# A hybrid encoder layer in split fp32: the norm moved from x to the columns, on GpSimd

## The chip, the cores and the metric

The kernel runs on one core of a Trainium2 chip. The metric is the device time of one execution in microseconds (us), as the median of several runs. TensorE (PE) multiplies matrices, VectorE (DVE) and ScalarE (ACT) work element by element, GpSimd (POOL) does the same more slowly and issues DMAs of its own, SyncE (SP) issues most of the others. Each engine takes its instructions strictly in the order in which the program lists them.

## What is computed

One layer, 512 tokens, 2048 channels, 12 heads in three branches (A forgetting attention, B chunked attention, C stick-breaking attention), all in float32:

```python
hn = rmsnorm(x, norm_g)                      # x * rsqrt(mean(x*x) + EPS) * norm_g
proj = einsum('bsd,dc->bsc', hn, w_in)       # 12 x (q, k, v, gate), 4 forget logits, 3 x 2048 gate columns
f_logit = proj[..., QKVG_COLS:QKVG_COLS + N_HEADS] + b_f
gates = sigmoid(proj[..., QKVG_COLS + N_HEADS:] + b_gate)
# A: q, k normed per head; logits + c[q] - c[k], c = cumsum(log_sigmoid(f_logit)); causal softmax
# B: q, k normed; learned bias by distance; softmax over a band
# C: causal, weights exp(z + sum of log(1 - beta) over the keys between)
ys = heads * silu(gate path)
up = einsum('bsnw,nwd->bsnd', ys, w_up)
out = x + einsum('bsd,de->bse', sum(gates * up), w_out)
```

The row factor rsqrt(mean(x*x) + EPS) of a token multiplies every column of that token's projection alike, so it can be put on x or on the columns. norm_g belongs to the channel, which is summed over, and has to be on x (or on the weights).

## The kernel before

Tokens lie on the free axis, channels or columns on the 128 partitions. A float32 operand is split in two parts that TensorE takes at full rate: hi is a rounded copy (ScalarE, `split`), lo the rest (VectorE). A product is hi x hi + hi x lo + lo x hi. A column block (128 columns of w_in) has 16 channel tiles (k-tiles), each with three matmuls over 512 tokens: 48 matmuls.

Most column blocks are computed in twos (`PairTask`) by Strassen's scheme with seven products instead of eight. A product is a unit: 8 matmuls of weights hi over 512 columns (hi and lo of half the tokens side by side) and 8 of weights lo over 256. It needs sums of weight quarters (two by VectorE, two by a DMA that GpSimd issues and that adds to the tile it writes, `add_up`, L278) and sums and differences of x quarters (`combos`). A pair's first form of product order is called late: it asks for the combinations of x as late as possible.

The order of the stages is this. x comes in 16 tiles; VectorE or ScalarE multiplies each by norm_g (`prep_x`, L422, L425), then it is split. With these the first head's four blocks, q, k, v and gate of (C, 0), are made plainly (`first_quad`), k-tile by k-tile, with one more matmul per k-tile and part for the forget logits (weights `w2`, 8 columns: hi and lo of four). Meanwhile ScalarE sums the squares of x (read again with tokens on the partitions, `norm_x`, L455), and one fp32 matmul (L470) spreads the row factors over all partitions (`rstd`). VectorE then multiplies x by rstd and splits it once more (`split_n`, L490); the quad's columns are multiplied by rstd as they leave PSUM (L1205). Four gate columns follow plainly (`col_task`), and during them VectorE and ScalarE make the combinations of x. From there on all is pairs: for each of eleven heads a q, k pair and a v, gate pair, between them pairs of gate columns (stored to memory, `spill`, and read back at the end), and the heads' attention in between. In branch A the running sum of the log forget gates is laid in two tiles (`forget_sums`), and a matmul per query block (L980) adds its differences to the logits. At the end come the up projections (units of w_up), the merge with the gates, and eight pairs of w_out.

The order of instructions on PE, ACT and DVE is written out by a planner (`Flow`): tasks are generators that yield an engine, an assumed cost and a due time, and the planner emits whichever can start first, then the one due first. POOL and SP instructions before the change keep an order of their own that a scheduler sets. Weight tiles: six raw ones (`NR`), splits made two units ahead (`LA`).

Of the kernel before, what the change touches and what calls it, by code (L numbers as in the profile page):

```python
# [15 lines left out]
P = 128  # L16
# [13 lines left out]
NEG = -1e30  # L30
SCALE = HD ** -0.5
# [4 lines left out]
PE, ACT, DVE = 0, 1, 2  # L36
# [26 lines left out]
class Flow:  # L63
# [5 lines left out]
    LATE = (0.3, 0.12, 0.12)  # L69

    def __init__(self):
        self.clock = [0.0] * 3
        self.idle = [0.0] * 3
        self.now = self.fin = 0.0
        self.tasks = []
# [84 lines left out]

@with_exitstack
def hybrid_kernel(
# [4 lines left out]
    consts: bass.AP,  # L167
    w_col: bass.AP,
# [152 lines left out]
    ohf = cp.tile([P, NH], F32, name="ohf")  # L321
    nc.gpsimd.memset(ohf, 0.0)
    for r in range(4):
        nc.gpsimd.affine_select(out=ohf[32 * r:32 * r + 32, :], in_=ohf[32 * r:32 * r + 32, :],
                                pattern=[[1, NH]], base=0, channel_multiplier=-1,
                                compare_op=ALU.not_equal, fill=1.0)

    gq = cp.tile([P, 4], F32, name="gq")
    nc.vector.tensor_copy(gq, gqk)
    for c in (0, 2):  # L330
        nc.vector.tensor_scalar_mul(gq[:, c:c + 1], gqk[:, c:c + 1], SCALE)

    w2 = cp.tile([P, KT, 2 * NH], F32R, name="w2")
    nc.vector.tensor_copy(w2[:, :, :NH], wf)
    nc.vector.tensor_sub(w2[:, :, NH:], wf, f(w2[:, :, :NH]))
# [4 lines left out]
                                                  mybir.EngineType.DVE}))  # L340
# [56 lines left out]
    norm_ev = [Event() for _ in range(KT)]  # L397
    used_q = [Event() for _ in range(KT)]
    used_g = [Event() for _ in range(UK)]
    x1 = [Parts("x1", [norm_ev[k], Event()]) for k in range(UK)]  # L400
    x2 = [Parts("x2", [norm_ev[k + UK]] * 2) for k in range(UK)]
# [5 lines left out]
    atts.free.pop()  # L407
    xps.free.clear()


    xnat = [xp.tile([P, 2, S], F32, tag="x", name=nm("xn")) for _ in range(UK)]
# [3 lines left out]
    def prep_x(kt):  # L415

        due = (5.0 + 3.2 * kt,)
        yield x_in[kt]
        x = xraw[kt]
        if kt < 10:  # L420
            yield (DVE, 0.5, *due)
            nc.vector.tensor_scalar_mul(x, x, gn[:, kt:kt + 1])  # L422
        else:
            yield (ACT, 0.65, *due)
            nc.scalar.activation(x, x, AF.Copy, scale=gn[:, kt:kt + 1])  # L425
        yield from split(xs[kt].hi, xs[kt].lo, two(x), S, raw_ev[kt], due, raw_hi[kt])
# [19 lines left out]
    rstd, rstd_ev = [], Event()  # L446
    n_split = [0]

    def norm_x():

        for i in range(NQ * QB):
            yield n_in[i]
            yield ACT, 0.75, 12.0 + 1.5 * i
            x = xnat[i // 2][:, i % 2, :]
            nc.scalar.activation(x, x, AF.Square, accum_out=ssq[:, i // NQ, i % NQ:i % NQ + 1])  # L455
        give(xps, UK)
# [15 lines left out]
        yield t2s, 1  # L472
        yield ACT, act_us(S)
        rstd.append(t2("rstd"))
        nc.scalar.activation(rstd[0], ps, AF.Copy)
# [3 lines left out]
    def rstd_used():  # L479
        n_split[0] += 1  # L480
        if n_split[0] == KT + 5:
            give(t2s)

    def split_n(kt):

        due = (52.0 + 1.0 * kt + (8 if kt >= UK else 0),)
        yield raw_ev[kt]
        yield rstd_ev
        yield (DVE, dve_us(S), *due)
        nc.vector.tensor_mul(xraw[kt], xraw[kt], rstd[0])  # L490
        yield used_q[kt]
        yield from split(xs[kt].hi, xs[kt].lo, two(xraw[kt]), S, norm_ev[kt], due)
        rstd_used()

    def combos(k):

        due = (96.0 + k,)
        late = (106.0 + k,)
        a, b = xraw[k], xraw[k + UK]
        yield norm_ev[k]  # L500
        yield norm_ev[k + UK]
        q = dve_us(HS)
        yield (DVE, q, *due)
        nc.vector.tensor_sub(a[:, LH], a[:, LH], a[:, RH])
        yield (DVE, q, *due)
        nc.vector.tensor_sub(a[:, RH], b[:, RH], a[:, RH])
        yield (DVE, q, *due)
        minus(b[:, RH], b[:, RH], a[:, LH])
        yield (DVE, q, *due)
        minus(b[:, LH], b[:, RH], b[:, LH])  # L510
        yield used_g[k]
        h, lo, ev = x1[k].half(1)
        yield from split(h, lo, a[:, LH], HS, ev, due)
        yield xps, 1
        t23[k] = Parts("t23")
        h, lo, ev = t23[k].half(0)
        yield from split(h, lo, b[:, RH], HS, ev, late)
        h, lo, ev = t23[k].half(1)
        yield from split(h, lo, a[:, RH], HS, ev, late)
        give(t2s)  # L520
# [21 lines left out]

    def col_task(srcs, evac, bank=0, used=None):

        st = {}

        def mms(i):
            def go(u):
                if i == 0:
                    yield accs[bank], 1  # L550
                    st["ps"] = acc(bank)
                ps = two(st["ps"])
                for j in range(UK):
                    kt = i * UK + j
                    yield norm_ev[kt]
                    yield PE, mm_us(S, 2)
                    mm(ps, u.hi[:, j, :], xs[kt].hi, kt == 0)
                    mm(ps, u.hi[:, j, :], xs[kt].lo)
                yield u.ready
                for j in range(UK):  # L560
                    kt = i * UK + j
                    yield PE, mm_us(S)
                    mm(ps, u.lo[:, j, :], xs[kt].hi, stop=kt == KT - 1)
                    if used is not None and i == 0:
                        set_(used[j])
            return go

        def after():
            yield from evac(st["ps"])
            give(accs[bank])  # L570
        return [Unit(mms(i), after if i == 1 else None, srcs=[srcs[i]]) for i in range(2)]
# [20 lines left out]
    class PairTask:  # L592
# [204 lines left out]
    bias, bias_ev, f_ev, f2_ev = {}, Event(), Event(), Event()  # L797
    fd, fd2 = dp.tile([2 * NH, S], F32, name="fd"), dp.tile([NH, S], F32, name="fd2")

    def forget_bias():  # L800
# [5 lines left out]
        nc.sync.dma_start(v, fd[:NH, :].rearrange("h (c t) -> (h c) t", t=T))  # L806
        nc.sync.dma_start(u, fd[NH:, :].rearrange("h (c t) -> (h c) t", t=T))
        yield Event(f_ev.t + 6.0)
        q = 0.15
        yield DVE, q  # L810
        nc.vector.scalar_tensor_tensor(v, v, bfc, u, op0=ALU.add, op1=ALU.add)
        yield DVE, q
# [13 lines left out]
        yield DVE, 3 * q  # L826
        nc.vector.scalar_tensor_tensor(p, p, 1.0, s, op0=ALU.add, op1=ALU.mult)
        nc.vector.tensor_scalar_mul(p, p, 2.0)
        nc.vector.scalar_tensor_tensor(v, v, 0.0, p, op0=ALU.min, op1=ALU.subtract)
        nc.sync.dma_start(fd2.rearrange("h (c t) -> (h c) t", t=T), v)  # L830
        f2_ev.t = flow.fin + 3.0

    def forget_sums():
        yield f2_ev
        yield t2s, 3
        v, s, u = t2("fv"), t2("fs"), t2("fu")
        nc.gpsimd.memset(v, 0.0)
        nc.gpsimd.memset(u, 1.0)
        for r in range(4):
            nc.sync.dma_start(v[32 * r:32 * r + NH, :], fd2)  # L840
        yield Event(flow.now + 6.0)
        yield DVE, 1.2
        nc.vector.tensor_tensor_scan(s, u, v, 0.0, op0=ALU.mult, op1=ALU.add)
        give(t2s)
        yield t2s, 2
        hi, lo = pair_of("c")
        yield from split(hi, lo, s, S)
        give(t2s)
        yield t2s, 2
        crl, crb = t2("crl", F32R), t2("crb")  # L850
        a = ACT, act_us(S)
        yield a
        nc.scalar.activation(crl[0:32, :], f(hi[0:32, :]), AF.Copy)
        yield a
        nc.scalar.activation(crl[32:64, :], f(lo[32:64, :]), AF.Copy)
        yield a
        nc.scalar.activation(crl[64:128, :], u[64:128, :], AF.Copy)
        nc.gpsimd.memset(crb[0:64, :], 1.0)
        yield a
        nc.scalar.activation(crb[64:96, :], f(hi[64:96, :]), AF.Copy, scale=-1.0)  # L860
        yield a
        nc.scalar.activation(crb[96:128, :], f(lo[96:128, :]), AF.Copy, scale=-1.0)
        give(t2s, 3)
        bias["crl"], bias["crb"] = crl, crb
        set_(bias_ev)
# [8 lines left out]
    class Head:  # L874
# [73 lines left out]
        def soft_start(self):  # L948
# [18 lines left out]
        def soft_scores(self, i):  # L967
# [6 lines left out]
            yield PE, mm_us(m, 3) + (mm_us(m) + mm_us(P) if n == A else 0)  # L974
# [4 lines left out]
            if n == A:  # L979
                nc.tensor.matmul(ps, bias["crl"][:, blk(i)], self.bias[:, :m], start=False, stop=False)  # L980
                nc.tensor.matmul(ps[:, blk(i)], identb, mska, start=False, stop=True)
                done = self.nth("s", QB)
                yield DVE, dve_us(m)
# [605 lines left out]
```

## Time and profile before

| | |
|---|---|
| median of 3 runs | 1350.9 us (1350.63 to 1351.42) |
| the profiled execution | 1351.0 us, span from first to last instruction 1349.3 us |
| granted TensorE clock, mean | 0.997 |
| busy: PE, DVE, ACT, POOL | 1326.0, 1108.8, 797.3, 93.5 us |
| first real matmul | 9.96 us |
| quad ends, four plain gate columns end | 64.38, 107.89 us |
| data moved by DMA | 262.00 MB, 194 GB/s on average |

In rows of the profile, L12 is line 12 of the kernel, `out<-in` are the program's tile names, `x16` is a count. In a group's row the busy time and the mean ns of one come first, then the idle time of the engine before them and what ended it. A timeline's row begins with start and length in us. Columns of a windows row: busy time (and instructions) of PE, weight loads, DVE, ACT, POOL, then granted clock, DMA share, GB/s. [...]

### The profile page before, as it was taken

The numbers are of one execution on the slowest core, as the hardware profiler recorded it, in microseconds if no ns is written. First come the engines' busy times: TensorE is split into PE (matmuls) and PEld (weight loads), VectorE is DVE, ScalarE is ACT, GpSimd is POOL, SyncE is SP. The second block draws the span as 40 slices with busy tenths as digits, with TensorE's granted clock in tenths as the row PEclk, the third lists the DMA queues.
The fourth block names the chain that finished last, engine by engine and source line by source line (L and its number), as shares of the span: only waits on it lengthen the run. The fifth ranks groups of instructions, "written<-read, shape, count | busy, mean of one in ns | idle before, by whom it ended". The sixth has DMA issues, their size and how long they took to land.

```text
span 1349.3 us, 19660 instructions
## 1 busy us (share of the span) xinstructions
PE 1326.0 (98%) x7338; PEld 1149.2 (85%) x7338; DVE 1108.8 (82%) x1589; ACT 797.3 (59%) x1224; POOL 93.5 (7%) x123
## 2 busy tenths in 40 slices
PE   7999999999999999999999999999999999989998
PEld 5788888888888888888888888888888788878887
DVE  5998998978878788787888878878787877898786
ACT  6755756656565576655767557665567645454443
POOL 0000000010000000000110000100000000000000
PEclk9999999999999999999999999999999999989999
DMA  9556766667767677777777777777767655758893
GB/s 327 173 143 157 194 171 181 187 195 194 187 196 202 183 212 183 187 204 183 212 174 190 193 194 196 167 193 186 192 184 250 246 192 179 209 134 245 236 250 89
DMA packets 91055, 262.00 MB, mean 194 GB/s; under 512 B 10168, under 2 KB 16440, under 8 KB 90960
## 3 DMA queue, kind: packets, MB, share of 16 engines
q1 hardware_dynamic: 72384, 201.96, 44.6%
q0 software_dynamic: 14976, 54.53, 24.7%
q10 hardware_dynamic: 3600, 4.26, 0.9%
q8 instruction: 57, 0.93, 0.3%
q14 instruction: 38, 0.31, 0.1%
HBM read 241.03 MB, written 19.69 MB: 193 GB/s over the span
## 4 chain that ended last, share of the span: by engine, by line
PE 96%; DVE 3%; DMA 0%; issue 0%; ACT 0%; SPq 0%; DVEq 0%; ACTq 0%
PE acc L262 82%; PE att L262 8%; PE att L1013 1%; DVE wl L247 1%; DVE m L247 1%; PE att L1116 1%; PE att L258 1%; PE att L1117 1%; PE att L259 1%; PE att L257 1%; PE att L1115 1%; DMA x<-in_xT 0%; PE att L1076 0%; PE att L911 0%; PE att L912 0%
## 5 line engine op out<-in xcount | busy, mean ns | idle before, releaser
L247 DVE TENSOR_TENSOR wl<-raw,wh 128x1024 fp32r<-128x1024 f32 (+1 forms) x412 | 494.2, 1200 | 149.7 <-ACT wh L243 148.8
L243 ACT ACTIVATE wh<-raw 128x1024 fp32r<-128x1024 f32 (+1 forms) x412 | 427.1, 1038 | 149.8 <-PE acc L262 69.5
L262 PE MATMUL acc<-x,wh 128*128 128x512 f32 x1600 | 416.1, 396 | 10.0 <-ACT wh L243 10.0
L262 PEld LDWEIGHTS acc<-x,wh 128*128 128x128 f32 x1600 | 287.0, 189 | 62.0 <-ACT wh L243 10.0
L262 PE MATMUL acc<-t,wh 128*128 128x512 f32 x1056 | 272.7, 395 | 0.2 <-ACT wh L243 0.2
L262 PEld LDWEIGHTS acc<-x,wl 128*128 128x128 f32 x1504 | 210.6, 190 | 18.9
L262 PE MATMUL acc<-x,wl 128*128 128x256 f32 (+1 forms) x1504 | 223.7, 289 | 0.0
L262 PEld LDWEIGHTS acc<-t,wh 128*128 128x128 f32 x1056 | 188.0, 189 | 31.9 <-ACT wh L243 0.4
L262 PEld LDWEIGHTS acc<-t,wl 128*128 128x128 f32 x1056 | 145.0, 190 | 11.0
L262 PE MATMUL acc<-t,wl 128*128 128x256 f32 x1056 | 148.6, 282 | 0.0
L278 POOL DMA_DIRECT2D raw<-in_w_col x88 | 76.1, 865 | 934.7 <-DMA raw<-in_w_col 429.1
L262 PE MATMUL acc<-m,wh 128*128 128x512 f32 x448 | 113.8, 396 | 6.4 <-DVE m L247 6.0
L262 PEld LDWEIGHTS acc<-m,wh 128*128 128x128 f32 x448 | 81.6, 191 | 21.6 <-DVE m L247 6.4
L746 ACT ACTIVATE c<-acc 128x256 f32<-128x256 f32 x50 | 19.2, 384 | 105.4 <-PE acc L262 100.4
L724 ACT ACTIVATE u<-acc 128x512 f32<-128x512 f32 x50 | 29.8, 596 | 66.6 <-PE acc L262 66.5
L262 PE MATMUL att<-y,wh 128*128 128x512 f32 x256 | 66.5, 391 | 1.3 <-DVE y L247 1.3
L262 PEld LDWEIGHTS acc<-m,wl 128*128 128x128 f32 x448 | 61.9, 193 | 5.1 <-DVE wl L247 0.8
L636 DVE TENSOR_TENSOR raw<-raw,raw 128x1024 f32<-128x1024 f32 x52 | 63.5, 1221 | 0.4
L630 DVE TENSOR_TENSOR raw<-raw,raw 128x1024 f32<-128x1024 f32 x52 | 63.4, 1220 | 0.4
L262 PE MATMUL acc<-m,wl 128*128 128x256 f32 x448 | 63.4, 285 | 0.4 <-DVE wl L247 0.4
L707 ACT ACTIVATE v<-acc 128x512 f32<-128x512 f32 x52 | 31.1, 599 | 49.4 <-PE acc L262 46.1
L262 PEld LDWEIGHTS att<-y,wh 128*128 128x128 f32 x256 | 47.9, 188 | 12.2 <-DVE y L247 2.5
(193 smaller groups left out, 1371.9 us busy)
## 6 DMA issues: line engine op xcount, KB each, us to landing
raw<-in_w_col SPq DMA_DIRECT2D x236, 512.0 KB, 4.4
raw<-in_w_col POOLq DMA_DIRECT2D x88, 512.0 KB, 6.4
raw<-in_w_out SPq DMA_DIRECT2D x40, 512.0 KB, 4.4
gl<-c SPq DMA_DIRECT2D x48, 256.0 KB, 2.2
raw<-in_w_up SPq DMA_DIRECT2D x32, 384.0 KB, 3.1
sg<-gl SPq DMA_DIRECT2D x48, 256.0 KB, 5.1
raw<-in_w_out POOLq DMA_DIRECT2D x16, 512.0 KB, 6.8
x<-in_xT SPq DMA_DIRECT2D x16, 256.0 KB, 7.0
```

The lines of the kernel that those rows point to most:

```text
L243: nc.scalar.activation(hi, src, AF.Copy)
L247: nc.vector.tensor_sub(lo, src, f(hi))
L257: nc.tensor.matmul(ps, lh, rh, start=start, stop=False, skip_group_check=more)
L258: nc.tensor.matmul(ps, lh, rl, start=False, stop=False, skip_group_check=more)
L259: nc.tensor.matmul(ps, ll, rh, start=False, stop=stop, skip_group_check=more)
L262: nc.tensor.matmul(ps, w, x, start=start, stop=stop, skip_group_check=more)
L278: nc.gpsimd.dma_start(to, src, accum_op=ALU.add)
L630: nc.vector.tensor_add(w[1], w[1], w[5])
L636: nc.vector.tensor_add(w[2], w[2], w[1])
L707: nc.scalar.activation(self.v, ps, AF.Copy)
L724: nc.scalar.activation(self.u, ps, AF.Copy)
L746: nc.scalar.activation(c, ps[:, RH], AF.Copy, scale=-1.0)
```

## The change

- x enters all products with norm_g alone. `prep_x` gives hi and lo in one instruction each; `split_n` is gone. What leaves a pair is multiplied by rstd (now a tile of its own) on GpSimd (`scaled`, L485 of the new file; the quad's four blocks and the logits at L1159 and L1172, after a copy out of PSUM by ScalarE).
- The four plain gate columns are gone: two more pairs take their place, the first of them (late form) right behind the quad. `combos` works on x without its norm during the quad, two of its steps on GpSimd, in an order of k-tiles (`KORD`) that brings k and k + 8 together.
- The forget logits are fp32 matmuls of 4 weight columns, four k-tiles at a time in four strips (`tile_position`) that write partitions 0, 32, 64 and 96 of one PSUM bank; the four partial sums are added later. `w2` is gone.
- Branch A's bias is a running sum per head, read from memory spread over the partitions (`cr`), scanned by VectorE, and added while the maximum is taken, as in branch B. `forget_sums` and the matmul at L980 are gone. (The row's own term c[q] cancels in the softmax.)
- The quad's weights come in an array of their own (`w_first`), in nine pieces, the first two of one k-tile. 68 matmuls of 128 columns on a constant run before everything, into the bank of the logits, which VectorE then clears.
- The planner now also sets the order of POOL and SP. The adding DMAs are a planned POOL instruction (`added`).

```diff
+WARM = 68
...
-    LATE = (0.3, 0.12, 0.12)
+    LATE = (0.3, 0.12, 0.12, 0.2)
...
+def pool_us(n, x=1):
+    return x * (0.2 + 0.0022 * n)
...
-    w2 = cp.tile([P, KT, 2 * NH], F32R, name="w2")
-    nc.vector.tensor_copy(w2[:, :, :NH], wf)
-    nc.vector.tensor_sub(w2[:, :, NH:], wf, f(w2[:, :, :NH]))
+    nc.vector.tensor_tensor(wf, wf, gn.unsqueeze(2).to_broadcast([P, KT, NH]), op=ALU.mult)
...
-                                                  mybir.EngineType.DVE}))
+                                                  mybir.EngineType.DVE, mybir.EngineType.Pool,
+                                                  mybir.EngineType.SP}))
...
+    for _ in range(WARM):
+        nc.tensor.matmul(first_ps[:, :P], identb, identb, start=True, stop=True)
+    nc.vector.memset(first_ps, 0.0)
...
     def prep_x(kt):
...
-        yield from split(xs[kt].hi, xs[kt].lo, two(x), S, raw_ev[kt], due, raw_hi[kt])
+        x, g = xraw[kt], gn[:, kt:kt + 1]
+        yield (ACT, act_us(S), *due)
+        nc.scalar.activation(xs[kt].hi, two(x), AF.Copy, scale=g)
+        set_(raw_hi[kt])
+        yield (DVE, dve_us(S), *due)
+        nc.vector.scalar_tensor_tensor(xs[kt].lo, two(x), g, f(xs[kt].hi), op0=ALU.mult, op1=ALU.subtract)
+        set_(raw_ev[kt])
...
-    def split_n(kt):
-
-        due = (52.0 + 1.0 * kt + (8 if kt >= UK else 0),)
-        yield raw_ev[kt]
-        yield rstd_ev
-        yield (DVE, dve_us(S), *due)
-        nc.vector.tensor_mul(xraw[kt], xraw[kt], rstd[0])
-        yield used_q[kt]
-        yield from split(xs[kt].hi, xs[kt].lo, two(xraw[kt]), S, norm_ev[kt], due)
-        rstd_used()
+    def scaled(then):
+
+        def go(c):
+            yield rstd_ev
+            yield POOL, pool_us(S)
+            nc.gpsimd.tensor_mul(c, c, rstd)
+            yield from then(c)
+        return go
...
     def combos(k):
...
+        yield (POOL, 0.9, *due)
+        nc.gpsimd.tensor_scalar_mul(a, a, ga)
         yield (DVE, q, *due)
-        nc.vector.tensor_sub(a[:, LH], a[:, LH], a[:, RH])
+        mul_sub(nc.vector, b[:, RH], b[:, RH], gb, a[:, RH])
+        yield (POOL, pool_us(HS), *due)
+        nc.gpsimd.tensor_sub(a[:, RH], a[:, LH], a[:, RH])
...
-    def col_task(srcs, evac, bank=0, used=None):
...
                 if len(srcs) > 1:
-                    ev = add_up(t, srcs[1], ev.t, 512)
-                self.there[p].t = ev.t
+                    spawn(self.added(p, srcs[1], ev), 1.0)
+                else:
+                    self.there[p].t = ev.t
...
+        def added(self, p, src, ev):
+            yield ev
+            yield POOL, 0.9
+            self.there[p].t = add_up(self.w[p], src, flow.fin, 512).t
...
-    def forget_sums():
...
             if n == A:
-                yield bias_ev
-                self.bias = t2("cr", F32R)
-                yield ACT, act_us(S)
-                nc.scalar.activation(self.bias, bias["crb"], AF.Copy, scale=ohf[:, self.h:self.h + 1])
+                yield f2_ev
+                b = self.bias = t2("cr")
+                ev = fetch(b, fd2[self.h:self.h + 1, :].to_broadcast([P, S]), flow.now, 256)
+                yield ev
+                yield DVE, dve_us(2 * S)
+                nc.vector.tensor_tensor_scan(b, b, b, 0.0, op0=ALU.add, op1=ALU.max)
...
-                nc.tensor.matmul(ps, bias["crl"][:, blk(i)], self.bias[:, :m], start=False, stop=False)
                 nc.tensor.matmul(ps[:, blk(i)], identb, mska, start=False, stop=True)
...
+                for g, first in ((0, 4), (1, 6), (2, 8), (3, 10)):
+                    if at == first:
+                        four = KORD[4 * g:4 * g + 4]
+                        for kt in four:
+                            yield x_in[kt]
+                        yield PE, 1.0
+                        for j, kt in enumerate(four):
+                            nc.tensor.matmul(first_ps[32 * j:32 * j + NH, :], wf[:, kt, :], xraw[kt],
+                                             start=g == 0, stop=g == 3, tile_position=(0, 32 * j))
...
-                        if part < 2:
-                            mm(two(first_ps[:2 * NH, :]), w2[:, kt, :], x, kt + part == 0, kt + part == KT)
...
         def take(r):
             def go():
                 yield t2s, 1
-                yield DVE, dve_us(S)
+                yield ACT, act_us(S)
                 c = t2("c")
-                nc.vector.tensor_mul(c, ps[r], rstd[0])
+                nc.scalar.activation(c, ps[r], AF.Copy)
                 give(atts if r in (V, G) else accs[0])
-                rstd_used()
+                yield rstd_ev
+                yield POOL, pool_us(S)
+                nc.gpsimd.tensor_mul(c, c, rstd)
...
-        cols = []
-        for _ in range(2):
-            g, d = gates.pop(0)
-            cols += [(g, d), (g, d + 1)]
-        t = [col_task(gate_col(*c), spilled(*c), b, used_g if i == 3 else None)
-             for i, (c, b) in enumerate(zip(cols, (1, 2, 0, 0)))]
-        for i in range(2):
-            units.extend(u[i] for u in t)
         at(OFF["fb"], forget_bias)
         gate_units(late=True)
+        gate_units()
...
+        units.extend(PairTask(col(n, Q, h), col(n, K, h), ops, scaled(hd.got(Q)), None, scaled(hd.got(K))).units)
+        if not last:
             gate_units()
...
+NQ_U = 9
+KORD = [i // 2 + UK * (i % 2) for i in range(KT)]
```

Three places show how the instructions move. First TensorE in the quad (`acc` and `att` of four numbers are the four blocks, `wh` and `wl` the parts of the weights, `x` followed by two numbers a split x, by one number a raw x). Before, its first rows:

```order
L262 MATMUL acc_224<-x_2_126,wh_214 128x512
L262 MATMUL acc_225<-x_2_126,wh_214 128x512
L262 MATMUL att_226<-x_2_126,wh_214 128x512
L262 MATMUL att_227<-x_2_126,wh_214 128x512
L262 MATMUL att_142<-x_2_126,w_121 8x512
L262 MATMUL acc_224<-x_3_127,wh_214 128x512
```

Now, between the quad's third and fourth unit:

```order
L268 MATMUL att_263<-x_11_121,wl_257 128x512
L268 MATMUL att_264<-x_11_121,wl_257 128x512
L1132 MATMUL att_128<-x_202,small_in 4x512
L1132 MATMUL att_128<-x_206,small_in 4x512
L1132 MATMUL att_128<-x_210,small_in 4x512
L1132 MATMUL att_128<-x_212,small_in 4x512
L268 MATMUL acc_261<-x_4_114,wh_293 128x512
```

A logit matmul behind every fourth matmul has become a group of four on raw x, at four places in the quad. Second, TensorE where the quad now ends (`acc_728` is the first unit of the first pair):

```order
L268 MATMUL att_264<-x_9_119,wl_551 128x512
L268 MATMUL acc_261<-x_17_127,wl_551 128x512
L268 MATMUL acc_262<-x_17_127,wl_551 128x512
L268 MATMUL att_263<-x_17_127,wl_551 128x512
L268 MATMUL att_264<-x_17_127,wl_551 128x512
L268 MATMUL acc_728<-x_2_112,wh_611 128x512
L268 MATMUL acc_728<-x_3_113,wh_611 128x512
```

Before, the rows behind the quad were the plain gate columns, two matmuls per k-tile in 16 k-tiles and four blocks; now the pair follows at once. Third, GpSimd behind the quad (`c` are finished columns, `raw` weight tiles). Before, adding DMAs alone:

```order
L278 DMA raw_652<-in_w_col 128x1024
L278 DMA raw_766<-in_w_col 128x1024
L278 DMA raw_873<-in_w_col 128x1024
L278 DMA raw_1085<-in_w_col 128x1024
L278 DMA raw_1139<-in_w_col 128x1024
```

Now:

```order
L1159 TENSOR_TENSOR c_739<-c_739,rstd 128x512
L1172 TENSOR_TENSOR f_744<-f_744,rstd 128x512
L284 DMA raw_833<-in_w_col 128x1024
L485 TENSOR_TENSOR c_120_825<-c_120_825,rstd 128x512
L284 DMA raw_861<-in_w_col 128x1024
L485 TENSOR_TENSOR c_134_911<-c_134_911,rstd 128x512
L284 DMA raw_1019<-in_w_col 128x1024
L284 DMA raw_1068<-in_w_col 128x1024
```

Products and adding DMAs share the queue, in turn. On SP the stores of gate columns, which follow those products, stand between weight fetches as they did before.

More of the change, by code (lines that the diff above doesn't have):

```diff
@@ L35 @@
 Q, K, V, G = 0, 1, 2, 3
-PE, ACT, DVE = 0, 1, 2
+PE, ACT, DVE, POOL = 0, 1, 2, 3
 MARGIN = 0.25
@@ L516, in combos @@
         h, lo, ev = t23[k].half(0)
+        yield from split(h, lo, a[:, LH], HS, ev, late)
+        give(t2s)
+        h, lo, ev = t23[k].half(1)
         yield from split(h, lo, b[:, RH], HS, ev, late)
-        h, lo, ev = t23[k].half(1)
-        yield from split(h, lo, a[:, RH], HS, ev, late)
-        give(t2s)
         if k % 2 == 0:
@@ L541, in halves @@
         return [w_col[c, 0], w_col[c, 1]]
-    def col_task(srcs, evac, bank=0, used=None):
[L545 to L571, printed above, removed]
     class Pair(Unit):
@@ L825, in forget_bias @@
             nc.vector.scalar_tensor_tensor(p, p, 1.0 / (2 * k + 1), u, op0=ALU.add, op1=ALU.mult)
-        yield DVE, 3 * q
+        yield DVE, 4 * q
         nc.vector.scalar_tensor_tensor(p, p, 1.0, s, op0=ALU.add, op1=ALU.mult)
         nc.vector.tensor_scalar_mul(p, p, 2.0)
-        nc.vector.scalar_tensor_tensor(v, v, 0.0, p, op0=ALU.min, op1=ALU.subtract)
+        nc.vector.tensor_scalar(v, v, -1.0, 0.0, op0=ALU.mult, op1=ALU.max)
+        nc.vector.tensor_add(v, v, p)
         nc.sync.dma_start(fd2.rearrange("h (c t) -> (h c) t", t=T), v)
         f2_ev.t = flow.fin + 3.0
-    def forget_sums():
[L834 to L865, printed above, removed]
     def tri(name, dt=F32):
@@ L1531, in hybrid_kernel @@
     spawn(norm_x(), 5.0)
-    for kt in range(KT):
-        spawn(split_n(kt), 5.0)
     for k in range(UK):
```

186 lines of the change are left out of this document (84 added, 102 removed).

## The prediction

> **What bounds the kernel now.** I read the page first: busy shares and the chain that ended last.
>
> ```profile
> PE 1326.0 (98%) x7338; PEld 1149.2 (85%) x7338; DVE 1108.8 (82%) x1589; ACT 797.3 (59%) x1224; POOL 93.5 (7%) x123
> PE 96%; DVE 3%; DMA 0%; issue 0%; ACT 0%; SPq 0%; DVEq 0%; ACTq 0%
> ```
>
> TensorE is busy for all but 23.3 us of the span and is 96% of the chain. So time is won only by fewer or shorter matmuls, or by closing its few gaps. The waits of TensorE name them:
>
> ```profile
> PE acc L262 <- ACT wh L243: 10.6, 3, 10.0
> PE acc L262 <- DVE m L247: 6.0, 1, 6.0
> PE att L262 <- DVE y L247: 1.3, 2, 1.0
> PE att L1013 <- ACT p L1065: 1.0, 1, 1.0
> ```
>
> 10.0 us of this is the start; the 6.0 and 1.3 us stand late, in stages whose code the change leaves alone, and I keep them. The rest is the tail after the last matmul. So I read the start row by row (timeline of PE, then of the others):
>
> ```profile
> 9.96 1.22 PE L262 MATMUL acc<-x,wh 128*128 128x512 f32 x2 [9.96 <-ACT wh L243]
> 10.98 1.05 PE L262 MATMUL att<-x,wh 128*128 128x512 f32 x2
> 11.84 0.63 PE L262 MATMUL att<-x,w 128*8 128x512 f32 x1
> 14.40 0.67 PE L262 MATMUL acc<-x,wh 128*128 128x512 f32 x2
> 18.57 0.62 PE L262 MATMUL acc<-x,wh 128*128 128x512 f32 x2
> 19.48 0.40 PE L262 MATMUL att<-x,w 128*8 128x512 f32 x1
> 19.72 0.62 PE L262 MATMUL acc<-x,wh 128*128 128x512 f32 x2
> 37.82 1.02 PE L470 MATMUL att<-dg,tmpc 128*128 128x512 f32 x2
> 39.14 0.62 PE L262 MATMUL att<-x,wh 128*128 128x512 f32 x2
> 64.38 3.79 PE L262 MATMUL acc<-x,wh 128*128 128x512 f32 x16
> 107.89 1.98 PE L262 MATMUL acc<-x,wh 128*128 128x512 f32 x8
> 116.25 2.00 PE L262 MATMUL acc<-x,wh 128*128 128x512 f32 x8
> ```
>
> Starts are exact, ends modelled, so I use distances between starts. A full-speed matmul with 512 moving columns costs (19.48 - 18.57)/4 = 0.2275 us. Until 14.40 it costs twice that: the two of 10.98 take 0.86 us. A forget-logit matmul, though only 8 weight columns wide, costs 19.72 - 19.48 = 0.24 us. The plain fp32 matmul of L470 is two records; 37.82 to 39.14 holds it and two others, so it costs 1.32 - 0.455 = 0.87 us. The first four columns (the quad) end at 64.38, the four plain gate columns at 107.89, and from there a unit of a Strassen pair takes (116.25 - 107.89)/3 = 2.79 us.
>
> **The change part by part.** The sum is made against the profiled execution, 1351.0 us, 0.1 over the median of the runs.
>
> *The start and the quad.* 68 matmuls of 128 columns now run first. They need only identb:
>
> ```profile
> 1.66 0.29 DVE L310 CAST identb<-identf 128x128 bf16<-128x128 f32 x1 [0.32 <-POOL identf L307]
> 5.71 0.17 DVE L329 COPY gq<-small_in 128x4 f32<-128x4 f32 x1 [3.52 <-DMA small_in<-in_consts]
> 7.82 0.48 DVE L422 TENSOR_SCALAR x<-x,small_in 128x512 f32<-128x512 f32 x1 [1.55 <-DMA x<-in_xT]
> 8.33 0.63 ACT L243 ACTIVATE x<-x 128x512 fp32r<-128x512 f32 x1 [6.25 <-DVE x L422]
> 8.87 1.04 ACT L243 ACTIVATE wh<-raw 128x1024 fp32r<-128x1024 f32 x1
> ```
>
> They start near 2.1. At the slow rate 128 columns cost 0.43/4 = 0.107 us; the slow stretch lasted 14.40 - 9.96 = 4.4 us, so 41 run slow. The other 27 cost between 0.054 (twice as fast) and 0.11 us (a 128-column matmul in the L980 rows below): the loop ends between 8.0 and 9.5. The data is there at about the same time: x landed at 7.8 behind 512 KB of weights and now goes first with weights of half that size; then ScalarE splits both, 0.63 + 0.6 us. I take 8.8 for the first real matmul. VectorE clears the logit bank only after the loop (0.5 us, as GpSimd's memset of that shape below) and then makes the low part of x (0.69); TensorE has four matmuls (0.9 us) meanwhile: 0.4 us of waiting. Then 192 x 0.2275 = 43.7, L473 0.9, and the new logit matmuls S.
>
> S is what the trace does not show. 16 fp32 matmuls replace 32 x 0.24 = 7.7 us. Bounds: one after another, 16 x 0.87 = 13.9; four strips fully side by side, 4 x 0.87 = 3.5. The four of a group use 4 weight columns each and write partitions 0, 32, 64 and 96, so they share nothing that I can name except the instruction queue. I take the low end and 0.15 per group for starting: 4.1. [...]
>
> The quad ends at 8.8 + 0.4 + 43.7 + 0.9 + 4.1 = 57.9 instead of 64.38: **-6.5** (with the ends of start and S -7.9 to +4).
>
> *Plain columns to pairs.* 107.89 - 64.38 = 43.5 us go; two more pairs come, 14 x 2.79 = 39.0: **-4.5**. The pair needs the combinations of x some 40 us sooner; they no longer wait for the norm, and are done on GpSimd and VectorE during the quad, where VectorE loses the norm's products (first row) and half of the x splits:
>
> ```profile
> L490 DVE TENSOR_TENSOR x<-x,rstd 128x512 f32<-128x512 f32 x16 | 10.3, 688 | 0.7 <-ACT rstd L475 0.7
> 40.00:50.00 10.00, 10.00 (x45) 7.44 (x45) 10.00 (x15) 9.56 (x16) 0.00 (x0) 1.00 0.79 281
> 50.00:60.00 10.00, 10.00 (x45) 7.64 (x44) 10.00 (x16) 5.94 (x9) 0.00 (x0) 1.00 0.19 61
> ```
>
> (VectorE full there.) New is that the pair's first unit uses a bank that the quad held, so TensorE waits for a copy of 0.6 us begun four matmuls before the quad's end, and that ScalarE's copies push the splits behind it: **+0.5** (0 to 1.5).
>
> *FoX bias.* 16 bias matmuls go. First and last of their sizes:
>
> ```profile
> 756.13 0.27 PE L980 MATMUL att<-cr,crl 128*128 128x128 f32 x1
> 756.24 0.23 PE L981 MATMUL att<-mska,identb 128*128 128x128 bf16 x1
> 766.88 0.39 PE L980 MATMUL att<-cr,crl 128*128 128x512 f32 x1
> 767.11 0.23 PE L981 MATMUL att<-mska,identb 128*128 128x128 bf16 x1
> ```
>
> 0.11 to 0.23, mean 0.17: **-2.7**. VectorE's add-and-maximum with its read costs as much as the maximum it replaces plus 0.1 us, the four scans 1.2 us each; both are small beside its idle time.
>
> *The norm on the columns.* 97 products of 128x512 on GpSimd: 92 behind pairs, 5 after the quad. Its nearest rows, with VectorE's load behind:
>
> ```profile
> L1580 POOL MEMSET const-float32-0.0<- 128x1 f32 x1 | 0.1, 103 | 0.3 <-issue 0.3
> L838 POOL MEMSET fu<- 128x512 f32 x1 | 0.5, 527 | 0.0
> L318 POOL TENSOR_SCALAR_AFFINE_SELECT mskc<-tmpc 128x128 f32<-128x128 f32 x1 | 0.3, 287 | 0.0
> 160.00:200.00 40.00, 39.79 (x235) 35.10 (x235) 38.48 (x73) 25.43 (x43) 3.44 (x4) 1.00 0.71 185
> 200.00:300.00 100.00, 99.01 (x580) 87.25 (x579) 84.43 (x114) 58.08 (x88) 7.77 (x9) 1.00 0.69 190
> 400.00:600.00 200.00, 200.00 (x1160) 176.36 (x1159) 166.22 (x245) 121.86 (x185) 16.40 (x19) 1.00 0.73 195
> 559.81 3.26 PE acc L262 x20
> 644.34 3.26 PE acc L262 x20
> ```
>
> A write alone is 0.53 us; the select's slope, (287 - 103)/128 = 1.4 ns an element with the smallest op at 103 ns, gives 0.85 for one input, 1.6 for two. I take 1.2: 116 us on an engine busy for 94. The chain view's two like pieces put a head at 84.5 us, with eight products, 9.6 us of GpSimd. Columns wait 1.2 us more, which the gates (stored and read 300 us and more later) do not feel. What can be felt is VectorE: 83% busy from 400 to 600, 70.2 of 84.5 us, 14.3 free. If each product costs VectorE its length, it rises to 94%. Where it stood at 96%, 160 to 200, TensorE lost 0.2 us there and 1.0 at 202: 1.2 per head, 13 over eleven. So 0 to 13; I take **+2.5**, since VectorE gives TensorE's next-but-one weights and most delays fit in that lead. [...]
>
> Sum: -6.5 - 4.5 + 0.5 - 2.7 + 2.5 = -10.7; 1351.0 - 10.7 = **1340.3 us**.
>
> **The rivals.**
>
> *Strips overlap by half.* The fp32 matmul is two records, and in order the second of one strip must end before that strip is free; neighbours then overlap by one half: 5 x 0.435 = 2.2 us a group, S = 8.7: 1344.9. For: the x2 of L470. *Strips do not overlap*: S = 13.9, 1350.1. That is the change not doing what it says. Against both: the strips share no columns and no partitions.
>
> *VectorE becomes the bound (the slower side).* Place: the heads, 120 to 1050. If GpSimd's products and VectorE's two-input work exclude each other, each product takes VectorE's time; from 14.3/8 = 1.8 us apiece VectorE no longer fits into a head. At 2.0 us (the 1.6 above, lengthened by waiting) a head grows by 1.7 us, eleven by 19: 1351.0 - 13.2 + 19 = 1357. For: 83% already. [...] Short of that point, its 13 us give 1351.
>
> *GpSimd's queue stands in the way.* It now holds products and adding DMAs in one order, and SP's stores of gate columns wait for the products with weight fetches queued behind them:
>
> ```profile
> POOL raw L278 <- DMA raw<-in_w_col: 429.1, 39, 15.8
> SPq L1156 <- DVE c L692: 79.1, 20, 5.0
> ```
>
> A product behind an adding DMA that waits up to 15.8 us for its first half comes late, its store too, and the fetches. At 0.5 us for each of 24 gate pairs: 1340.3 + 12 = 1352. Against: after the start no split waits on a weight DMA in the waits view, although SP sat 79 us at these stores.
>
> **How the numbers follow.** Forecast 0.52 (its own range 1336 to 1343); half overlap 0.17; no overlap 0.09; VectorE near full 0.08, over full 0.06; queue 0.05; better than forecast 0.03 (a start at 8.0, no loss on VectorE, no gap at 202: -16). Range: from that -16, 1334, up to 1350, which takes in both cases of the strips and half of VectorE near full. A measurement here tells 0.2%, 2.7 us, from no change: below 1348.2 lie the forecast, half overlap, the better case and bits of the others, 0.77; within, 0.15; slower, 0.08.
>
> **What would show it.** First real matmul near 8.8, no doubled costs after it; quad's end near 58 (62 with half overlap, 68 without); the four strips of a group starting within some tenths of a us; first pair 39 us for two; no cr,crl matmul; GpSimd's products near 1.2 us, VectorE's 128x1024 splits still 1.22 us on average (more would be the exclusion); TensorE's waits on wl, 0.4 us now, at some us. The forecast is wrong if those waits pass 10 us, if SP or GpSimd wait lists show fetches late, or if the quad ends after 62.

## The result

The changed kernel takes **1375.8 us** (median; 1374.4 to 1377.3) against 1351.0 for the kernel before on the same chip: a ratio of 1.0184, 95% interval 1.0169 to 1.0198. It is 25 us slower, where 11 us faster was forecast. Both the time and the sign were wrong; the range, which ended at 1350, missed by 26 us.

The page of the changed kernel (busy us, share of the span, instructions):

```profile
PE 1335.6 (97%) x7422; PEld 1151.9 (84%) x7422; DVE 1190.7 (87%) x1597; ACT 788.2 (57%) x1208; POOL 288.7 (21%) x232
PE 24%; DVE 3%; ACT 1%; issue 1%; DMA 0%; SPq 0%; DVEq 0%
```

The profiled run took 1377.3 us with a span of 1375.1. VectorE runs eight instructions more than before and is busy 82 us longer; so its instructions became longer (the groups below show which). GpSimd gained 195 us. TensorE's waits, by what it waited for (total, times, longest):

```profile
PE acc L268 <- DVE m L253: 5.9, 1, 5.9
PE att L1018 <- DVE al L253: 4.8, 2, 2.4
PE att L264 <- DVE qkl L253: 4.5, 8, 1.2
PE acc L268 <- DVE wl L253: 2.8, 3, 1.6
PE att L955 <- DVE al L253: 2.5, 2, 2.2
PE att L473 <- ACT dg L469: 2.4, 1, 2.4
PE att L955 <- ACT p L944: 1.8, 6, 0.5
```

Of these only the first, and 0.4 us on `wl`, stood in the list of before. The others are low parts of queries, keys and transposed probabilities that VectorE finished late (`qkl`, `al`), the probabilities themselves, and the norm at the end of the quad. The groups name what became longer: the 128x1024 sums (`raw<-raw,raw`) and splits (`wl<-raw,wh`), all at 1.22 us before (first view), and the products (second view, changed kernel).

```profile
L636 DVE TENSOR_TENSOR raw<-raw,raw 128x1024 f32<-128x1024 f32 x52 | 63.5, 1221 | 0.4
L630 DVE TENSOR_TENSOR raw<-raw,raw 128x1024 f32<-128x1024 f32 x52 | 63.4, 1220 | 0.4
L247 DVE TENSOR_TENSOR wl<-raw,wh 128x1024 fp32r<-128x1024 f32 x380 | 463.6, 1221 | 144.9 <-ACT wh L243 143.9 <-ACT x L243 0.2
```

```profile
L615 DVE TENSOR_TENSOR raw<-raw,raw 128x1024 f32<-128x1024 f32 x54 | 91.1, 1688 | 0.4
L609 DVE TENSOR_TENSOR raw<-raw,raw 128x1024 f32<-128x1024 f32 x54 | 70.2, 1301 | 0.4
L253 DVE TENSOR_TENSOR wl<-raw,wh 128x1024 fp32r<-128x1024 f32 x385 | 499.1, 1298 | 122.4 <-ACT wh L249 112.5 <-PE acc L268 9.4
L485 POOL TENSOR_TENSOR c<-c,rstd 128x512 f32<-128x512 f32 x92 | 171.1, 1876 | 203.5 <-DVE c L671 159.9 <-DVE c L727 21.9 <-issue 18.9
```

How one instruction lengthens another is seen in the timeline of the changed kernel around 266 us, here without the rows of other engines and of other instructions (start, duration, engine, line):

```profile
265.59 1.21 DVE L609 TENSOR_TENSOR raw<-raw,raw 128x1024 f32<-128x1024 f32 x1
265.74 2.20 POOL L485 TENSOR_TENSOR c<-c,rstd 128x512 f32<-128x512 f32 x1 [1.49 <-DVE c L727]
...
266.83 2.19 DVE L615 TENSOR_TENSOR raw<-raw,raw 128x1024 f32<-128x1024 f32 x1
...
268.94 0.68 DVE L253 TENSOR_TENSOR al<-att,ah 128x512 fp32r<-128x512 f32 x1
...
269.77 0.84 PE L1018 MATMUL att<-identf,c 128*128 128x128 f32 x4 [2.38 <-DVE al L253]
```

The sum of L609 ends at 266.80. The product began beside it and ends 1.14 us later, though it "took" 2.20. The sum of L615 began at 266.83 and ends at 269.02, 1.08 after the product, though it "took" 2.19. That is what is seen if each holds the other off for as long as it runs. Behind them `al` came late, and TensorE stood 2.38 us. Over the whole trace, 54 of VectorE's 128x1024 instructions began while a product ran; the median end is 1.08 us after the product's, and eight in ten lie between 1.080 and 1.093. A product that VectorE did not hold up took 1.29 us, so the mean of 1.88 is a third waiting:

```profile
786.19 1.29 POOL L485 TENSOR_TENSOR c<-c,rstd 128x512 f32<-128x512 f32 x1 [1.78 <-DVE c L727]
```

VectorE instructions that read PSUM beside SBUF were not lengthened: seven `al<-att,ah` of 128x256 and ten `c<-c,acc` ran beside a product in this trace, and both took 0.42 us in the median, as they do without one (0.42 and 0.41).

### The profile page after: what moved, and what is told of

It is laid out like the page before. It is cut to its first block, busy times and chain, and to the rows that moved or that the text cites. A ratio compares the mean times of both kernels' runs of the same rounds, so it can differ in the third digit from the quotient of the medians.

```text
span 1375.1 us, 20048 instructions
## 1 busy us (share of the span) xinstructions
PE 1335.6 (97%) x7422; PEld 1151.9 (84%) x7422; DVE 1190.7 (87%) x1597; ACT 788.2 (57%) x1208; POOL 288.7 (21%) x232
## 5 line engine op out<-in xcount | busy, mean ns | idle before, releaser
L253 DVE TENSOR_TENSOR wl<-raw,wh 128x1024 fp32r<-128x1024 f32 (+2 forms) x419 | 533.3, 1274 | 126.2 <-ACT wh L249 116.3
L249 ACT ACTIVATE wh<-raw 128x1024 fp32r<-128x1024 f32 (+2 forms) x419 | 433.1, 1037 | 127.6 <-PE acc L268 60.9
L268 PE MATMUL acc<-x,wh 128*128 128x512 f32 x1536 | 403.0, 396 | 1.5 <-ACT wh L249 1.1
L268 PEld LDWEIGHTS acc<-x,wh 128*128 128x128 f32 x1536 | 274.0, 189 | 52.4 <-ACT wh L249 1.3
L268 PE MATMUL acc<-t,wh 128*128 128x512 f32 x1104 | 285.0, 397 | 2.4 <-DVE v L707 1.4
L268 PEld LDWEIGHTS acc<-t,wh 128*128 128x128 f32 x1104 | 198.3, 190 | 38.1 <-ACT wh L249 2.6
L485 POOL TENSOR_TENSOR c<-c,rstd 128x512 f32<-128x512 f32 x92 | 171.1, 1876 | 203.5 <-DVE c L671 159.9
L268 PE MATMUL acc<-t,wl 128*128 128x256 f32 x1104 | 156.3, 282 | 1.6 <-DVE wl L253 1.6
L615 DVE TENSOR_TENSOR raw<-raw,raw 128x1024 f32<-128x1024 f32 x54 | 91.1, 1688 | 0.4
L609 DVE TENSOR_TENSOR raw<-raw,raw 128x1024 f32<-128x1024 f32 x54 | 70.2, 1301 | 0.4
L284 POOL DMA_DIRECT2D raw<-in_w_out x16 | 13.8, 862 | 262.0 <-DMA sg<-gl 110.8
```

The costliest lines, as they stand in the source:

```text
L249: nc.scalar.activation(hi, src, AF.Copy)
L253: nc.vector.tensor_sub(lo, src, f(hi))
L268: nc.tensor.matmul(ps, w, x, start=start, stop=stop, skip_group_check=more)
L284: nc.gpsimd.dma_start(to, src, accum_op=ALU.add)
L485: nc.gpsimd.tensor_mul(c, c, rstd)
L609: nc.vector.tensor_add(w[1], w[1], w[5])
```

## The experiments

What a product costs can be its hold on VectorE (**lock**), its result coming late (**lateness**), or an order that was laid out for shorter products (**order**). All runs below change the new kernel unless it is said otherwise; ratios are to the kernel before on the same chip, with 95% intervals.

### Lock or lateness

*No product.* Edit, the same at the three places where a product stands:

```
-            nc.gpsimd.tensor_mul(c, c, rstd)
```

> The changed kernel with the 97 GpSimd products left out (columns stay without the norm's factor), everything else and the order of every engine as it was. Lock theory (a product and VectorE's instructions with two SBUF inputs shut each other out) and lateness theory (columns reach their consumers 1.9 us later) expect the same here: the prediction's sum without its last term, about 1338 us, 1336 to 1343, with VectorE's 128x1024 subtraction back at 1.22 us on average (1.30 in the changed kernel). If the loss sits in the new order itself, or in the combinations on GpSimd, the time stays above 1355.

Measured: 1345.1 us, 0.9950 (0.9935 to 0.9965); the subtraction is back at 1.22 us. So the products cost 30.7 us of the 1375.8, and the rest of the change gains 6. That is less than the 13 us forecast for it; the last experiment returns to this.

*Writes of the same length.*

```
-            nc.gpsimd.tensor_mul(c, c, rstd)
+            for part in (c, c, c, c[:, LH]):
+                nc.gpsimd.memset(part, 0.5)
```

> Each product replaced by GpSimd writes onto the same column (three and a half memsets of 128x512, about 1.9 us together; the columns become constants), same order. Columns are as late as with the product, but GpSimd reads no SBUF. Lock theory: within 4 us of the kernel without products, about 1340, VectorE's 128x1024 subtraction at 1.22 to 1.24 us. Lateness theory: stays near 1375.

Measured: 1344.7 us, 0.9952 (0.9934 to 0.9971). GpSimd is as busy as with the products (300.9 us against 288.7) and VectorE's durations are untouched (groups of this run):

```profile
L486 POOL MEMSET c<- 128x512 f32 x368 | 186.1, 507 | 230.9 <-DVE c L672 190.5 <-ACT y L249 15.0 <-DVE c L728 8.5
L616 DVE TENSOR_TENSOR raw<-raw,raw 128x1024 f32<-128x1024 f32 x54 | 65.9, 1220 | 0.4
```

Columns that come 2 us late (186.1 us of writes for 92 columns), in a queue with the adding DMAs, cost nothing (1344.7 us against 1345.1 without products). Lateness falls, and with it the rival of GpSimd's queue.

*Products that nobody waits for.* First the column times itself, then the column plus the norm's tile, both written onto the norm's tile:

```
-            nc.gpsimd.tensor_mul(c, c, rstd)
+            nc.gpsimd.tensor_mul(rstd, c, c)        # first run
+            nc.gpsimd.tensor_add(rstd, c, rstd)     # second run
```

> Each product replaced by the column times itself, written onto the tile of the norm, which nobody reads any more (columns stay without the factor), same order. GpSimd reads SBUF as before, but nobody waits for its result. Lock theory: near the changed kernel, 1365 to 1376, VectorE's 128x1024 subtraction near 1.30 us on average. Lateness theory: near the kernel without products, about 1340.

Measured: 1356.4 us, 1.0046 (1.0027 to 1.0065): between the two expectations. The groups showed that this instruction was not the product's equal; it reads one tile twice and was shorter (1.64 us against 1.88). So the second run reads two tiles:

> As the run with products set aside, but column plus norm tile, written onto the norm tile (columns stay without the factor): two different SBUF inputs, as the real product has, where the earlier run read one tile twice and was shorter (1.64 instead of 1.88 us). If the missing 19 us come from the longer hold of a two-tile product, 1368 to 1376; if they come from somebody waiting for a product that is itself held up, 1356 to 1361.

Measured: 1374.3 us, 1.0173 (1.0154 to 1.0192).

```profile
L485 POOL TENSOR_TENSOR rstd<-c 128x512 f32<-128x512 f32 x92 | 150.6, 1637 | 219.2 <-DVE c L671 192.0 <-DVE c L727 24.6 <-DVE c L259 2.0
L485 POOL TENSOR_TENSOR rstd<-c,rstd 128x512 f32<-128x512 f32 x92 | 174.3, 1894 | 210.9 <-DVE c L671 179.3 <-DVE c L727 28.4 <-DVE c L259 2.6
L615 DVE TENSOR_TENSOR raw<-raw,raw 128x1024 f32<-128x1024 f32 x54 | 88.2, 1633 | 0.4
```

(first row: the run with the column twice; the other two: the run with two tiles.) With two tiles, nobody waiting for a result, practically all of the loss is back: 29.2 of 30.7 us, with intervals that overlap those of the changed kernel. So the lock accounts for it, without anybody waiting for a product. The two runs also show how steep it is: VectorE's instructions beside GpSimd's are longer by 66 us in all in the first and by 90 in the second (each against the median of its kind alone; 7 us of both stand in the run without products too, beside the combinations of x), and the kernel by 11.3 and by 29.2. Some 5 us of that difference are the clock (last section): the mean granted clock of the runs is 0.996 in the first, as without products, and 0.993 in the second.

### How many products

```
-            nc.gpsimd.tensor_mul(c, c, rstd)
+            if gate:                    # the other run: if not gate
+                nc.gpsimd.tensor_mul(c, c, rstd)
```

> Only the 48 products of gate columns are kept, whose result nobody needs for hundreds of us; the 49 of the heads and of the logits are left out (their columns stay without the factor); same order. Lock alone: half of the 11.3 us that all products set aside cost over none, 1345.1 + 5.6 = 1351; if the whole 30.7 us go by the number of products, 1360.

> Only the 49 products of the heads' columns and of the logits are kept; the 48 of the gate columns are left out (these stay without the factor); same order. Lock plus waiting for held-up columns: the half of the lock, 5.6, and all of the interplay, 19.4, on 1345.1: 1370; by the number of products 1360.

Measured: 1356.6 us (1.0043; 1.0027 to 1.0059) with the gates' 48, 1352.4 us (1.0010; 1.0000 to 1.0020) with the heads' 49. Both theories of the expectation missed: neither is it the heads' urgency, nor does it go by number. Alone, the halves cost 11.5 and 7.3 us; together 30.7. Beside the products VectorE is lengthened by 45 and 43 us, in the changed kernel by 94. One us of lengthening costs 0.26 and 0.17 us of time in the halves, 0.33 in the whole. A small part is read from the clock (last section): spells of 3.41 us at half clock, 1.7 us lost in each, number one without products, two in each half and four in the whole. The whole has one more than the halves add up to, 1.7 of the 11.9 us that are missing. For the rest I can only argue that VectorE's slack takes up the first delays and is missing for the next; no run separates that, and it stays open.

### The order, and VectorE in GpSimd's place

```
 def pool_us(n, x=1):
-    return x * (0.2 + 0.0022 * n)
+    return x * (0.2 + 0.0033 * n)
...
-        yield (POOL, 0.9, *due)
+        yield (POOL, 1.95, *due)
```

> The changed kernel with the order planned for the measured lengths (a product 1.89 us instead of 1.33, a 128x256 subtraction 1.04 instead of 0.76, a scaling 1.95 instead of 0.9); the result is the reference's. If an order that came too early for the products made the interplay worth 19 us (1375.8 against 1356.4), most of that goes: 1356 to 1362. If VectorE's stretching sets the time whatever the order, 1370 to 1378.

Measured: 1377.2 us, 1.0191 (1.0161 to 1.0222). The order's costs are not the cause: an order laid out for the true length of a product knows nothing of what it does to VectorE.

```
-            yield POOL, pool_us(S)
-            nc.gpsimd.tensor_mul(c, c, rstd)
+            yield DVE, dve_us(S)
+            nc.vector.tensor_mul(c, c, rstd)
```

> The 97 products on VectorE, 0.69 us each as the products of this shape before, and the order planned with that. VectorE's work grows by 67 us, of which the changed kernel loses about 100 to stretching: lock theory expects 1340 to 1348, with all VectorE shapes at their durations of before. Lateness theory: 0.7 instead of 1.9 us of delay, so a third of the loss stays, about 1351. If any load on VectorE costs TensorE its length, 1360 or more.

Measured: 1349.9 us, 0.9997 (0.9987 to 1.0006). VectorE is busy 1158.8 us and no shape is longer than before. This is a little above the lock's range and inside what the lateness theory allowed, but that theory has fallen above. Against the run without products VectorE has 55 us more of planned work (1104.2 there), which cost 4.8 us, where 84 us of unplanned lengthening (beside the products of the run with two tiles) cost 29. The likely reason, which no run isolates, is that the order can lay work out where it has room, and cannot do that with a wait it does not know. As a whole the change then gains nothing.

### The other parts, in the kernel before

Three runs put parts of the change into the kernel before, where the norm still goes into x (16 products on VectorE) and the plain gate columns stay. The first has the running sums:

```
+        b = self.bias = t2("cr")
+        ev = fetch(b, fd2[self.h:self.h + 1, :].to_broadcast([P, S]), flow.now, 256)
+        nc.vector.tensor_tensor_scan(b, b, b, 0.0, op0=ALU.add, op1=ALU.max)
...
-        nc.tensor.matmul(ps, bias["crl"][:, blk(i)], self.bias[:, :m], start=False, stop=False)
```

> The kernel before with one part of the change: FoX bias by running sums (four scans, add-and-maximum, no bias matmuls, no splits of the sums). Its term in the prediction was -2.7: 1348.3, 1347.5 to 1349.5. If VectorE's scans or the broadcast loads are felt: 1350 to 1352.

Measured: 1348.4 us, 0.9981 (0.9972 to 0.9991). As expected.

The second has the start: 68 early matmuls, `w_first`, x split in one instruction each, the fp32 strips. The norm's product takes norm_g with it, since x stays raw until then:

```
-        nc.vector.tensor_mul(xraw[kt], xraw[kt], rstd[0])
+        nc.vector.scalar_tensor_tensor(xraw[kt], xraw[kt], gn[:, kt:kt + 1], rstd[0], op0=ALU.mult, op1=ALU.mult)
```

> The kernel before with another part of the change: the early matmuls, weights of the first head in the order of x, high and low parts of x made from raw x in one instruction each, fp32 forget logits in four strips. The norm still goes into x (16 products on VectorE, four plain gate columns). The prediction's term for start and quad was -6.5: 1344.5, 1343 to 1347. If the norm arrives late for the quad as in the changed kernel (a wait of 2.4 us and 3.41 us at half the clock), 1348 to 1350.

Measured: 1343.1 us, 0.9939 (0.9925 to 0.9954): at the lower end of the first range, 7.7 us gained.

> Both parts together, no GpSimd products and no column without norm: 1351.0 - 6.5 - 2.7 = 1341.8, 1340 to 1345; faster than both kernels, and about the changed kernel without its products (1345.1), since the plain gate columns cost 4.5 us more and the wait for the norm may be gone. If the two gains do not add, 1345 to 1348.

Measured: **1340.2 us, 0.9923 (0.9906 to 0.9940)**, faster than both kernels, as expected. Its start in the timeline of PE; the last row is the quad's end:

```profile
18.88 1.04 PE L1149 MATMUL att<-x,small_in 128*4 128x512 f32 x8
25.54 1.04 PE L1149 MATMUL att<-x,small_in 128*4 128x512 f32 x8
57.17 3.79 PE L264 MATMUL acc<-x,wh 128*128 128x512 f32 x16
```

### No GpSimd work at all

Without products, two kinds of GpSimd work are left: in the combinations of x, beside the quad.

```
-        nc.gpsimd.tensor_scalar_mul(a, a, ga)
+        nc.scalar.activation(a, a, AF.Copy, scale=ga)
...
-        nc.gpsimd.tensor_sub(a[:, RH], a[:, LH], a[:, RH])
+        nc.vector.tensor_sub(a[:, RH], a[:, LH], a[:, RH])
```

> The changed kernel without products (columns stay without the norm's factor) and with the combinations' GpSimd work moved as well (scaling to ScalarE, difference to VectorE), so that GpSimd computes nothing after its constants. If the lock also makes the norm late at the end of the quad (a VectorE subtraction of 2.5 us beside a scaling), that wait of 2.4 us and the half clock after it go: 1345.1 - 4 = 1341, 1340 to 1343. If ScalarE and VectorE were late there for their own load, 1344 to 1347.

Measured: 1339.1 us, 0.9914 (0.9900 to 0.9929), 6 us under the run that left these on GpSimd and 1 us below the first range. What the run that left them there shows in the timelines of POOL, DVE and PE, in this order:

```profile
48.70 2.67 POOL L504 TENSOR_SCALAR x<-x,small_in 128x512 f32<-128x512 f32 x1
47.43 2.52 DVE L253 TENSOR_TENSOR wl<-raw,wh 128x1024 fp32r<-128x1024 f32 x1
```

```profile
PE att L473 <- ACT dg L469: 2.4, 1, 2.4
```

In the new run a subtraction of this shape takes 1.22 us, and this wait and the half clock behind it are gone. It is not a clean proof that the lock made the norm late: the new costs also put the norm's matmul behind the quad, 6 us later in the order. With or without products, then, the new order keeps one loss against the kernel before. Its last head's attention stands in the stage of the up-projections; between 1000 and 1100 us the distances of matmul starts exceed their usual ones by 6.2 us in the run without products, by 2.6 before.

## Why the prediction was wrong

**The norm on the columns, the step that failed.** The term was +2.5 with bounds 0 to 13; it measured **+30.7** (1375.8 - 1345.1). Its parts: the product's length was right (1.2 taken, 1.29 where VectorE did not hold it up). That a product might cost VectorE its length was named and is nearly what happened (84 us beside the 97 products of the run with two tiles, 94 in the changed kernel: 0.87 to 0.97 each). Wrong was the price of that in time. I read "1.2 per head, 13 over eleven" off one stretch where VectorE was 96% busy, called it the upper bound, and went near the lower end "since VectorE gives TensorE's next-but-one weights and most delays fit in that lead". The lead exists for `wl`, whose waits are 2.8 us. The waits that came are for `al` and `qkl`, 12 us, which TensorE needs at once, in a fixed order. In the profiles TensorE's idle time grows by 20 us against the run without products (39.5 against 19.3), three more spells at half clock cost 5, and some 7 of the 32 us between the two spans stand in no list. What the trace of before showed was VectorE's average load, and the loss does not go by it: from 400 to 600 us of the run with two tiles VectorE is 88% busy, and TensorE stands idle for 2.5 us, in the run without products not at all (first row: without products; us, then PE, PEld, DVE, ACT, POOL).

```profile
400.00:600.00 200.00, 200.00 (x1160) 176.22 (x1159) 164.56 (x247) 124.22 (x190) 16.43 (x19) 1.00 0.75 193
400.00:600.00 200.00, 197.46 (x1137) 173.29 (x1138) 175.47 (x231) 123.15 (x184) 47.28 (x36) 1.00 0.72 194
```

So the rival "VectorE becomes the bound" (0.06, 1357) had the place, the mechanism and the sign, and the wrong condition: it asked for a full VectorE, at 1.8 us of VectorE's time per product. It needed neither. The exclusion entered the sum only as 0 to 13 us and two rivals of 0.14 together, since no row of before showed it; the changed kernel's trace does (54 instructions that end 1.08 us after the product, in the median). Of the signs that the prediction gave, the splits' mean showed the exclusion (1.30 us instead of 1.22); the limit set for TensorE's waits on `wl`, 10 us, was not reached (2.8), because the loss came elsewhere.

**The start and the quad, -6.5.** The parts held: first real matmul at 8.21 (8.8 said), the four strips of a group side by side, 0.97 us a group (20.86 - 19.89). With the slower starts around a group it costs 1.18 (from 19.34 to 21.43, less four matmuls), so 4.7 in all where 4.1 was taken. The two rivals of half and no overlap fall. But in the changed kernel the quad ends at 62.8 instead of 57.9. The term had left out the norm's own chain, which is 2.4 us late for L473 and leaves the clock at half for 3.41 us. The change itself moved that chain: it fetches the second copy of x from 14.3 to 31.3 us instead of 4.9 to 22.6, and the norm's matmul stands at 58.2 instead of 37.8, at the quad's end, with a lengthened VectorE subtraction (2.51 us at 47.74) before it. The prediction's own limit for the quad's end, 62, was passed. In the kernel before with the same start the norm's matmul stands earlier (at 37.7 with the start alone), the quad ends at 57.2 (both parts) and 57.9 (start alone), and the start alone gains 7.7 us.

```profile
8.21 0.70 PE L268 MATMUL acc<-x,wh 128*128 128x512 f32 x2
...
19.89 1.04 PE L1132 MATMUL att<-x,small_in 128*4 128x512 f32 x8
20.86 0.73 PE L268 MATMUL acc<-x,wh 128*128 128x512 f32 x2
...
58.20 1.85 PE L473 MATMUL att<-dg,tmpc 128*128 128x512 f32 x2 [2.40 <-ACT dg L469]
62.81 2.11 PE L268 MATMUL acc<-x,wh 128*128 128x512 f32 x8
```

**FoX bias, -2.7.** Measured alone: -2.3 (0.19%, 0.09 to 0.28%). Right.

**Plain columns to pairs, -4.5.** Not measured alone. The run without any GpSimd work has all gains and no products, and is 1.1 us under the one with the plain columns kept, which is within the noise. In the profiles its up-projections begin 6.5 us earlier (1028.6 against 1035.1) and end 3.2 us later (1170.7 against 1167.5): the last head's attention stands in that stage, partly as work that is done earlier in the other kernel, partly as late starts. (Its profiled execution took 2.2 us more than its median.) The late starts were in no step.

**The sum.** 35.5 us lie between forecast and result: 28.2 from the products, 4.9 from the quad's end, and 2.4 for all else, which the last head's 3.6 (6.2 against 2.6) more than cover. The range's lower end, 1334, is 1335 by its own sum; nothing hangs on it.

## What to carry to other kernels

Work moved onto GpSimd was not free here, where it read SBUF beside a VectorE that had two-input work: most of its length came back as VectorE time (0.87 to 0.97 us of 1.29), and unplanned, which cost six times as much as the same products planned on VectorE (29 us against 4.8). Before such a move, ask what TensorE needs next from VectorE without a lead, not how busy VectorE is on average. Writes alone cost nothing here (1344.7 us against 1345.1). And where a factor can be put on the shared operand once (16 products on x, 1340.2 us), it may beat 97 on the results, which took 1349.9 us even on VectorE; these two kernels differ in the order of the gate columns as well.

## What the runs showed of the hardware

**Short waits and the clock.** A wait of 2.4 us at L473 was followed by 3.41 us at half clock in the changed kernel, and in another run a wait of 2.38 us at the same place was not. In the traces of both kernels the granted clock changes, past the start, only on a grid of 3.41 us. Windows on that grid, changed kernel first (us, PE busy, clock, DMA share, GB/s), then the run with the column twice:

```profile
55.00:58.41 3.41, 1.01 (x5) 1.00 0.27 84
58.41:61.83 3.42, 3.42 (x7) 0.50 0.89 137
61.83:65.24 3.41, 3.38 (x17) 1.00 0.47 171
```

```profile
53.18:56.59 3.41, 1.99 (x8) 1.00 0.57 166
56.59:60.00 3.41, 2.36 (x9) 1.00 0.56 79
60.00:63.41 3.41, 3.28 (x18) 1.00 0.77 229
```

In the first the wait lies in one window, TensorE is idle for 70% of it, and the next runs at half; in the second a boundary cuts it into 42% and 31%, and nothing follows. The four such spells of the changed kernel follow windows that were idle for 65 to 70%; its windows of 47 and 42% were not followed by one. In the traces of the two kernels, past the start, a window at full clock that was idle for 65% or more was followed by half clock each time, one of up to 48% never; they have none between. So the same wait cost 2.4 or 4.1 us by where it fell on the grid, which is not at the same place in every run (boundaries at 58.41 us in the first, 56.59 in the second).

**One tile read twice.** A GpSimd product of a tile with itself took 1.64 us on average, one of two tiles 1.89; that of the logits' tile, right behind the quad, 1.10 and 1.37 (the run with the column twice, the run with two tiles).
